# Attention's output accumulator in one PSUM bank, with three narrow products per token tile in place of a wide and a narrow one

## The chip, the cores and the metric

The kernel runs on one core of a Trainium2 chip. The metric is the device time of one execution in microseconds (us); three executions of the kernel before are shown, and one more that was profiled.

## What is computed

One block of a streaming encoder on 4096 tokens of width 1024: a normalisation, one projection, eight heads of causal attention with a forgetting gate (head width 64) beside four heads of chunkwise retention (head width 128), gates, an output projection, a second normalisation and the residual. The change touches the product of the attention weights with the values only:

```python
logits = jnp.einsum('bhqd,bhkd->bhqk', qb, kb) * scale
logits = logits + c[:, :, q0:q1, None] - c[:, :, None, :q1]
logits = jnp.where(kpos <= qpos, logits, -jnp.inf)
p = jax.nn.softmax(logits, axis=-1)
outs.append(jnp.einsum('bhqk,bhkd->bhqd', p.astype(vb.dtype), vb))
```

## The kernel before, in words

Matrix products run on TensorE in float16 with each operand split into a high and a low half, so that products of halves stand for a float32 product. The program order of every engine is written by Python generators; nothing is reordered afterwards. All results of TensorE go to tiles of one tag, `PS()`, with eight buffers, one for each bank of PSUM. A tile takes the bank that was given back first, and its first matmul waits until the last reader of the bank's former tile is done.

The stages: `phase_f0` (to about 400 us) projects for the first four heads. Then `attention()` runs over 64 items (8 heads by 8 blocks of 512 queries). Item (h, qb) has 4(qb + 1) steps, one for each 128 keys, 1152 steps in all. Between its steps the main loop puts pieces of other work, the fillers: the projection of the other four heads (`fill_f1`), the retention (`fill_r`) and the output projection (`fill_o`). Attention ends at about 2850 us and `fill_o` runs on alone.

A step of attention (lines 1116 to 1150) does this. Two matmuls make 128 keys by 512 queries of scores in a bank `st`; two banks are taken at a time, for two steps. ScalarE takes the exponential twice, as float32 (`pf`, L1140) and as float16 (`ph`, L1141); GpSimd subtracts them to `pl`, the low half (L308). `max_tile` (L983) computes scores of a later item once more in a bank of its own, and VectorE reduces them to row maxima `mrow` (L999); one or two such turns lie in each step. The step's `ph` and `pl` are queued in `pvq`.

In every fourth step, at `kt % 4 == 2`, `emit_pv` (L1046) is called four times and works off the four oldest entries. For each of the four tiles of 128 tokens it multiplies `pl` with 65 columns of the values `vt` (64 high halves and a column of ones, which sums the weights) and `ph` with all 129 columns (the 64 high halves, the ones, the 64 low halves). Each of these matmuls has its own weight load, since the attention weights are the stationary operand. Such a run of 32 matmuls is called a batch here. On the diagonal, where `i >= 0`, tiles before the i-th are left out: there a batch has 20 matmuls.

The results of an item accumulate in two banks, tiles 0 and 1 in the first, 2 and 3 in the second, at columns 0 and 256. An item's last batch holds its whole diagonal. When that batch has done `i == 1`, ScalarE copies the first bank to `ac` in SBUF, and at the last entry the second (L1070). Then `finish_item` (L1077) runs on VectorE: the reciprocal of the sums, the sum of the two 64-column parts, and the scaling. In the trace `ac` appears as `s`, and all of `tt` has the line L141, all of `mm` the line L104. The order of the work is set by costs that are written by hand: `emit_pv` counts as 88 for each tile of tokens (L1124), which the change leaves as it is.

Of the kernel before, what the change touches and what calls it, by code (L numbers as in the profile page):

```python
# [13 lines left out]
ALU = mybir.AluOpType  # L14
# [39 lines left out]
def kernel(  # L54
# [14 lines left out]
    nc = tc.nc  # L69
# [18 lines left out]
    def SB(tag, shape, dt=F32):  # L88
        cnt[0] += 1
        slot = SHARED.get(tag, tag)  # L90
        return sbp.tile(shape, dt, tag=slot, name=f"{tag}_{cnt[0]}", bufs=BUFS.get(slot, 1))

    def PS():
        cnt[0] += 1
        return psp.tile([128, 512], F32, tag="ps", name=f"ps_{cnt[0]}", bufs=8)
# [7 lines left out]
    def mm(o, lhsT, rhs, start, stop):  # L103
        nc.tensor.matmul(out=o, lhsT=lhsT, rhs=rhs, start=start, stop=stop, skip_group_check=True)  # L104

    def dma(o, i):
        nc.sync.dma_start(out=o, in_=i)  # L107
# [3 lines left out]
    def spawn(gen):  # L111

        if next(gen, None) is not None:
            chains.append(gen)
# [11 lines left out]
    def until(key):  # L126

        while key not in done:
            assert chains, key
            tick()  # L130

    def drain(gen):
        for _ in gen:
            pass
# [5 lines left out]
    def tt(o, a, b, op):  # L140
        nc.vector.tensor_tensor(out=o, in0=a, in1=b, op=op)  # L141

    def ts(o, a, s1, s2, op0, op1):
        nc.vector.tensor_scalar(out=o, in0=a, scalar1=s1, scalar2=s2, op0=op0, op1=op1)  # L144
# [776 lines left out]
    def load_ready():  # L921

        while cpos[0] < min(len(chunk_list), BUFS["kc"] + freed[0]) and is_stored(*chunk_list[cpos[0]]):
            load_chunk(*chunk_list[cpos[0]])
            cpos[0] += 1
# [21 lines left out]
    def load_x(n):  # L947
        if n >= len(items):
            return
        h, qb = items[n]  # L950
        while not is_stored(h, qb):
            push(h)
        xq = SB("xq", [128, 512], F16)
        dma(xq[0 : R2 + 64, :], QX[h, 0 : R2 + 64, qb * 512 : (qb + 1) * 512])
        xqs[n] = xq
        xloaded[n] = gstep[0]

    def load_lq(n):
        if n >= len(items):
            return  # L960
        h, qb = items[n]
        lq = SB("lq", [128, 512], F16)
        for w in range(2):
            dma(lq[(1 - w) * 64 : (2 - w) * 64], QX[h, R2 + w * 64 : R2 + (w + 1) * 64, qb * 512 : (qb + 1) * 512])
        z = SB("z1", [128, 4, 64])
        dma(z, ZD[h // 4][h % 4, :, 4 * qb : 4 * qb + 4, :])
        lqs[n] = (lq, z)
# [35 lines left out]
    def max_tiles(n):  # L1003

        while mdone[0] < len(mlist) and mlist[mdone[0]][0] <= n:
            max_tile()
            yield 1
# [27 lines left out]
    def attention():  # L1035
        load_ready()
        for n in range(4):
            if n not in xqs:
                load_x(n)
        if NB <= 4:  # L1040
            for n in range(2):
                load_lq(n)
                drain(max_tiles(n))
        pvq = []

        def emit_pv():  # L1046
            it, kt, i, ph, pl, first, last = pvq.pop(0)
            h, qb = items[it["n"]]
            _, vt = chunks_use[it["n"], kt]
            if first:  # L1050
                it["acc"] = [PS(), PS()]
            for t in range(max(0, i), 4):
                a = it["acc"][t // 2]
                o = (t % 2) * 256
                sl = slice(t * 128, (t + 1) * 128)
                v = vt[:, kt % 4, :]
                if first and t % 2 == 0:
                    mm(a[:, o : o + 129], ph[:, sl], v, True, False)
                    mm(a[:, o : o + 65], pl[:, sl], v[:, 0:65], False, i == t)
                else:  # L1060
                    mm(a[:, o : o + 65], pl[:, sl], v[:, 0:65], False, False)
                    mm(a[:, o : o + 129], ph[:, sl], v, False, i == t)
            if qb == NB - 1 and kt % 4 == 3:
                freed[0] += 1
            load_ready()
            if i == 1 or last:
                b = 0 if i == 1 else 1
                if b == 0:
                    it["ac"] = SB("s2", [128, 4, 129])
                nc.scalar.copy(  # L1070
                    out=it["ac"][:, 2 * b : 2 * b + 2, :],
                    in_=it["acc"][b].rearrange("p (t d) -> p t d", t=2)[:, :, 0:129],
                )
            if last:
                spawn(finish_item(it))

        def finish_item(it):  # L1077
            h, qb = items[it["n"]]
            ac = it["ac"]
            z = it["z"]  # L1080
            rec = SB("sm", [128, 4, 1])
            o = ac[:, :, 0:64]
            yield 1
            nc.vector.reciprocal(out=rec, in_=ac[:, :, 64:65])
            tt(o, o, ac[:, :, 65:129], ALU.add)
            yield 1
            ts(rec, rec, gsc[h // 4][1][:, KT + 2 : KT + 3], None, ALU.mult, ALU.bypass)
            tt(o, o, z, ALU.mult)
            yield 1
            tt(o, o, rec.to_broadcast([128, 4, 64]), ALU.mult)  # L1090
            for _ in range(3):
                yield 1
            dma(MX[qb][h // 2][:, :, (h % 2) * 64 : (h % 2) * 64 + 64], o)
            attn_done[h, qb] = True

        def max_rate(g):

            rate = 0.0
            for j in range(len(items)):
                if mdue[j] > mdone[0]:  # L1100
                    if j >= 4 and first_step[j - 4] > g + 16:
                        break
                    rate = max(rate, (mdue[j] - mdone[0]) / max(first_step[j] - LEAD - g, 1))
            return min(2, math.ceil(rate - 1e-9))

        chunks_use = {}
        mdue = [sum(4 * (items[i][1] + 1) for i in range(j + 1)) for j in range(len(items))]
        first_step = [0] + mdue
        for n, (h, qb) in enumerate(items):
            xq = xqs.pop(n)  # L1110
            lq, z = lqs.pop(n)
            it = dict(n=n, z=z)
            es = gsc[h // 4][0][:, KT + 4 : KT + 5]
            until(("m", n))
            steps = 4 * (qb + 1)
            for kt in range(steps):
                c, kk = kt // 4, kt % 4
                kc, vt = get_chunk(h, c)
                chunks_use[n, kt] = (kc, vt)
                cost = 0.0  # L1120
                if kt % 2 == 0:
                    if kt % 4 == 2 and len(pvq) >= 6:
                        for _ in range(4):
                            cost += 88 * (4 - max(0, pvq[0][2]))  # L1124
                            emit_pv()
                    sts = []
                    for j in (kt - 4 * qb, kt + 1 - 4 * qb):
                        p = PS()
                        if j >= 0:
                            mm(p[:, j * 128 : (j + 1) * 128], idb, maskT, True, False)  # L1130
                        sts.append(p)
                i = kt - 4 * qb
                q0 = max(0, i) * 128
                st = sts[kt % 2]
                mm(st[:, q0:512], kc[0 : R2 + 64, 1, kk * 128 : (kk + 1) * 128], xq[0 : R2 + 64, q0:512], i < 0, False)
                mm(st[:, q0:512], kc[:, 0, kk * 128 : (kk + 1) * 128], lq[:, q0:512], False, True)
                pf = SB("pf", [128, 512])
                ph = SB("ph", [128, 512], F16)
                pl = SB("pl", [128, 512], F16)
                nc.scalar.activation(out=pf[:, q0:512], in_=st[:, q0:512], func=AF.Exp, scale=es)  # L1140
                nc.scalar.activation(out=ph[:, q0:512], in_=st[:, q0:512], func=AF.Exp, scale=es)  # L1141
                ptt(pl[:, q0:512], pf[:, q0:512], ph[:, q0:512], ALU.subtract)
                pvq.append((it, kt, i, ph, pl, kt == 0, kt == steps - 1))
                cost += 2 * (512 - q0) * 0.42 + (56 if i >= 0 else 0)
                gstep[0] += 1
                for _ in range(max_rate(gstep[0])):
                    if max_ready():
                        max_tile()
                        cost += 216
                yield cost  # L1150
            drain(max_tiles(n + 1))
            load_x(n + 4)
            load_lq(n + 2)
        while pvq:
            emit_pv()
# [217 lines left out]
```

## Time and profile before

| | us |
|---|---|
| median of three executions | 3187.65 (3186.91 to 3191.37) |
| the profiled execution | 3185.68 |
| its span, first to last instruction | 3183.9 |
| TensorE busy | 3029.5 |
| VectorE busy | 2107.4 |
| ScalarE busy | 1889.9 |
| GpSimd busy | 1354.3 |

Engines: PE is TensorE's matmuls, PEld its weight loads, DVE is VectorE, ACT ScalarE, POOL GpSimd. A name with its operands reads out<-in. Matmuls are pipelined, so the duration of one (some 0.19 us for 65 columns) is longer than the distance from its start to the next one's start. The distance is what a run of them costs.

### The profile page before, as it was taken

To read this page: it belongs to the slowest core of one execution; us is meant where nothing else is said; L and a number is where in the kernel's file an instruction comes from. 1 tells how busy PE (TensorE), PEld (TensorE's weight loads), DVE (VectorE), ACT (ScalarE), POOL (GpSimd) and SP (SyncE) were. 2 spreads that over 40 slices of the span, in tenths; PEclk is the share of its full clock that TensorE was granted. 3 is DMA by queue.
4 is the path that set the end of the run, shared out by engine and by line. 5 is a ranking of instruction groups with operands and counts; after the bars stand their busy time and mean duration, and the time that the engine had idled before them with its cause. 6 is when DMAs were issued, how large, how long until landed. Compare 5 with 4: busy or idle time off the path is not lost.

```text
span 3183.9 us, 59454 instructions
## 1 busy us (share of the span) xinstructions
PE 3029.5 (95%) x22574; PEld 1780.5 (56%) x22575; DVE 2107.4 (66%) x4436; ACT 1889.9 (59%) x3572; POOL 1354.3 (43%) x1285
## 2 busy tenths in 40 slices
PE   8999989999999999999999998999999999889999
PEld 6667545555555555565555554555555555555554
DVE  6545577446556676777778768676867786645555
ACT  4333346676677666666667675667666766663332
POOL 0000024564555555555555564456445645550000
PEclk9999999999999999999999999999999999999999
DMA  6446743233244321211114122112111321124443
GB/s 188 144 163 162 201 112 90 67 86 91 65 104 119 78 61 53 65 51 53 59 54 106 46 83 85 52 39 82 55 38 44 110 62 43 56 67 139 139 139 119
DMA packets 266143, 284.10 MB, mean 89 GB/s; under 512 B 58976, under 2 KB 212192, under 8 KB 265856
## 3 DMA queue, kind: packets, MB, share of 16 engines
q1 hardware_dynamic: 265856, 280.30, 30.8%
q8 instruction: 177, 2.90, 0.4%
q14 instruction: 110, 0.90, 0.1%
HBM read 194.88 MB, written 88.74 MB: 89 GB/s over the span
## 4 chain that ended last, share of the span: by engine, by line
PE 75%; DVE 14%; issue 3%; ACT 3%; DMA 2%; POOL 2%; SPq 1%; POOLq 0%; DVEq 0%; ACTq 0%
PE ps L104 73%; DVE mrow L999 3%; DVE s L141 3%; DVE s L144 2%; DVE sm L141 1%; POOL pl L308 1%; ACT ph L1141 1%; ACT pf L1140 1%; PE ps L1196 1%; DMA rw<-in_w_in_dram 1%; DVE sm L144 1%; PE ps L349 1%; SPq L107 1%; DVE s L147 1%; DVE sm L147 1%
## 5 line engine op out<-in xcount | busy, mean ns | idle before, releaser
L308 POOL TENSOR_TENSOR pl<-pf,ph 128x512 f16<-128x512 f32 (+3 forms) x1152 | 1283.9, 1119 | 1164.1 <-ACT ph L1141 885.8
L1140 ACT ACTIVATE pf<-ps,gsc 128x512 f32<-128x512 f32 (+3 forms) x1152 | 758.4, 658 | 714.1 <-PE ps L104 696.9
L999 DVE TENSOR_REDUCE mrow<-ps 128x1 f32<-128x512 f32 (+3 forms) x1152 | 717.4, 640 | 366.9 <-PE ps L104 355.9
L104 PE MATMUL ps<-wn,xh 128*128 128x512 f16 (+2 forms) x3840 | 855.7, 360 | 3.7 <-DVE qk L147 3.4
L1141 ACT ACTIVATE ph<-ps,gsc 128x512 f16<-128x512 f32 (+3 forms) x1152 | 753.7, 654 | 0.0
L104 PEld LDWEIGHTS <-xh 128*128 128x128 f16 x4608 | 449.9, 98 | 461.7 <-issue 36.2
L104 PE MATMUL ps<-xh,wt 128*128 128x512 f16 x2688 | 672.9, 383 | 5.0 <-DVE mrow L999 4.6
L104 PEld LDWEIGHTS <-wt 128*128 128x128 f16 x3168 | 310.3, 99 | 365.9 <-issue 38.4
L104 PE MATMUL ps<-xq,kc 99*128 99x512 f16 (+3 forms) x1152 | 421.0, 366 | 27.1 <-DVE mrow L999 11.2
L104 PE MATMUL ps<-kc,xq 99*128 99x512 f16 (+3 forms) x1152 | 384.9, 365 | 45.6 <-DVE mrow L999 34.2
L104 PE MATMUL ps<-vt,ph 128*128 128x129 f16 x4224 | 420.4, 222 | 5.5 <-DVE mrow L999 4.9
L104 PE MATMUL ps<-lq,kc 128*128 128x512 f16 (+3 forms) x1152 | 420.0, 365 | 0.0
L104 PE MATMUL ps<-vt,pl 128*128 128x65 f16 x4224 | 405.9, 195 | 13.5 <-POOL pl L308 13.3
L104 PEld LDWEIGHTS <-kc 128*128 128x128 f16 (+1 forms) x3072 | 288.2, 99 | 213.9 <-issue 27.9
L104 PEld LDWEIGHTS <-pl 128*128 128x128 f16 x4224 | 375.2, 99 | 57.3 <-POOL pl L308 22.3
L104 PEld LDWEIGHTS <-ph 128*128 128x128 f16 x4224 | 377.4, 98 | 31.8 <-issue 1.6
L141 DVE TENSOR_TENSOR s<-s,s 64x512 f32<-64x512 f32 (+1 forms) x256 | 259.2, 1013 | 29.8 <-ACT s L755 22.7
L308 POOL TENSOR_TENSOR sm<-sm,nhalf 128x4 f32<-128x4 f32 (+2 forms) x80 | 62.9, 787 | 352.7 <-DVE sm L144 311.2
L104 PEld LDWEIGHTS <-xq 99*128 99x128 f16 x1152 | 112.4, 99 | 140.3 <-issue 13.5
L104 PE MATMUL ps<-wt,xh 128*128 128x512 f16 x768 | 183.0, 379 | 0.0
L141 DVE TENSOR_TENSOR ps<-ps,maskM 128x128 f32<-128x128 f32 x256 | 75.0, 293 | 105.6 <-PE ps L104 104.6
L141 DVE TENSOR_TENSOR xh<-ps,xh 128x256 f16<-128x256 f32 (+1 forms) x128 | 70.1, 555 | 104.0 <-ACT xh L338 84.5
(121 smaller groups left out, 2587.4 us busy)
## 6 DMA issues: line engine op xcount, KB each, us to landing
xh<-XT SPq DMA_DIRECT2D x176, 256.0 KB
rw<-in_w_in_dram SPq DMA_DIRECT2D x104, 256.0 KB
xt<-in_x_dram SPq DMA_DIRECT2D x36, 512.0 KB
s<-MX SPq DMA_DIRECT2D x32, 512.0 KB
out_dram<-xt SPq DMA_DIRECT2D x31, 512.0 KB
s<-in_x_dram SPq DMA_DIRECT2D x28, 512.0 KB
VD<-s SPq DMA_DIRECT2D x16, 516.0 KB
vt<-VD SPq DMA_DIRECT2D x64, 129.0 KB
```

Source lines behind the costliest of these rows:

```text
L104: nc.tensor.matmul(out=o, lhsT=lhsT, rhs=rhs, start=start, stop=stop, skip_group_check=True)
L107: nc.sync.dma_start(out=o, in_=i)
L141: nc.vector.tensor_tensor(out=o, in0=a, in1=b, op=op)
L144: nc.vector.tensor_scalar(out=o, in0=a, scalar1=s1, scalar2=s2, op0=op0, op1=op1)
L147: nc.vector.scalar_tensor_tensor(out=o, in0=a, scalar=s, in1=b, op0=op0, op1=op1)
L308: nc.gpsimd.tensor_tensor(out=o, in0=a, in1=b, op=op)
L349: nc.tensor.transpose(p[:, t * 128 : (t + 1) * 128], xs[t][:, k * 128 : (k + 1) * 128], idf)
L999: nc.vector.tensor_reduce(out=mrow[:, t, c : c + 1], in_=p[:, 0:w], axis=AX.X, op=ALU.max)
L1140: nc.scalar.activation(out=pf[:, q0:512], in_=st[:, q0:512], func=AF.Exp, scale=es)
L1141: nc.scalar.activation(out=ph[:, q0:512], in_=st[:, q0:512], func=AF.Exp, scale=es)
L1196: nc.tensor.transpose(p[:, e * 128 : (e + 1) * 128], mxt[:, half * 4 + e, :], idf)
```

## The change

Per token tile the wide product with `ph` is split in two of 65 and 64 columns, and both add into the same 64 columns. The sum of the two parts, which VectorE made at the end of an item, is thus made in PSUM. Four tiles of 65 columns fit one bank, so an item has one accumulator bank and one copy out of it, at its end. The products with `ph` now always come ahead of the one with `pl`. The matmul that opens the bank is the first of tile 0.

```diff
             if first:
-                it["acc"] = [PS(), PS()]
+                it["acc"] = PS()
+            a = it["acc"]
             for t in range(max(0, i), 4):
-                a = it["acc"][t // 2]
-                o = (t % 2) * 256
+                o = t * 65
                 sl = slice(t * 128, (t + 1) * 128)
                 v = vt[:, kt % 4, :]
-                if first and t % 2 == 0:
-                    mm(a[:, o : o + 129], ph[:, sl], v, True, False)
-                    mm(a[:, o : o + 65], pl[:, sl], v[:, 0:65], False, i == t)
-                else:
-                    mm(a[:, o : o + 65], pl[:, sl], v[:, 0:65], False, False)
-                    mm(a[:, o : o + 129], ph[:, sl], v, False, i == t)
+                start = first and t == 0
+                mm(a[:, o : o + 65], ph[:, sl], v[:, 0:65], start, False)
+                mm(a[:, o : o + 64], ph[:, sl], v[:, 65:129], False, False)
+                mm(a[:, o : o + 65], pl[:, sl], v[:, 0:65], False, i == t)
             if qb == NB - 1 and kt % 4 == 3:
                 freed[0] += 1
             load_ready()
-            if i == 1 or last:
-                b = 0 if i == 1 else 1
-                if b == 0:
-                    it["ac"] = SB("s2", [128, 4, 129])
-                nc.scalar.copy(
-                    out=it["ac"][:, 2 * b : 2 * b + 2, :],
-                    in_=it["acc"][b].rearrange("p (t d) -> p t d", t=2)[:, :, 0:129],
-                )
+            if last:
+                it["ac"] = SB("s2", [128, 4, 65])
+                nc.scalar.copy(out=it["ac"], in_=a[:, 0:260].rearrange("p (t d) -> p t d", t=4))
             if last:
                 spawn(finish_item(it))
...
             nc.vector.reciprocal(out=rec, in_=ac[:, :, 64:65])
-            tt(o, o, ac[:, :, 65:129], ALU.add)
             yield 1
```

## Rows read from the trace of the kernel before

**Rows 1.** The page: busy us, share of the span, instructions; chain that ended last.
```profile
PE 3029.5 (95%) x22574; PEld 1780.5 (56%) x22575; DVE 2107.4 (66%) x4436; ACT 1889.9 (59%) x3572; POOL 1354.3 (43%) x1285
PE 75%; DVE 14%; issue 3%; ACT 3%; DMA 2%; POOL 2%; SPq 1%; POOLq 0%; DVEq 0%; ACTq 0%
```
**Rows 2.** Busy us (instructions) of each engine, PEclk, DMA by stage.
```profile
500.00:1100.00 600.00, 598.30 (x4668) 330.69 (x4667) 334.93 (x657) 415.64 (x766) 327.61 (x311) 1.00 0.32 86
1100.00:2840.00 1740.00, 1627.63 (x12963) 968.04 (x12962) 1288.82 (x2522) 1163.26 (x2157) 956.99 (x851) 0.98 0.22 62
```
**Rows 3.** TensorE's waits, 1100:2840: total us, times, longest us.
```profile
PE ps L104 <- DVE mrow L999: 53.9, 46, 4.8
PE ps L104 <- POOL pl L308: 12.7, 6, 5.2
PE ps L1196 <- ACT s L1188: 8.4, 1, 8.4
PE ps L104 <- DVE state L147: 7.0, 7, 2.9
PE ps L811 <- DVE mrow L999: 3.2, 1, 3.2
```
**Rows 4.** Groups by form, whole span: count | busy us, mean ns | idle before.
```profile
L104 PE MATMUL ps<-vt,ph 128*128 128x129 f16 x4224 | 420.4, 222 | 5.5 <-DVE mrow L999 4.9 <-ACT ph L1141 0.5
L104 PE MATMUL ps<-vt,pl 128*128 128x65 f16 x4224 | 405.9, 195 | 13.5 <-POOL pl L308 13.3
L141 DVE TENSOR_TENSOR s<-s 128x256 f32<-128x256 f32 x64 | 47.2, 738 | 0.0
L1070 ACT COPY s<-ps 128x258 f32<-128x258 f32 x128 | 45.3, 391 | 15.3 <-PE ps L104 13.2
```
**Rows 5.** Matmuls of `vt` by stage: length, busy us (instructions), PEclk, DMA.
```profile
500.00:1100.00 600.00, 110.90 (x2228) 1.00 0.32 86
1100.00:2840.00 1740.00, 306.16 (x6012) 0.98 0.22 62
```
**Rows 6.** Timeline of a batch and the fill after it: start us, us, engine.
```profile
1505.00 0.19 PE L104 MATMUL ps<-vt,pl 128*128 128x65 f16 x1
1505.00 0.10 PEld L104 LDWEIGHTS <-ph 128*128 128x128 f16 x1
1505.03 0.22 PE L104 MATMUL ps<-vt,ph 128*128 128x129 f16 x1
1505.09 0.19 PE L104 MATMUL ps<-vt,pl 128*128 128x65 f16 x1
...
1506.41 0.38 PE L104 MATMUL ps<-xq,kc 99*128 99x512 f16 x1
...
1507.07 2.75 PE L104 MATMUL ps<-wn,xh 128*128 128x512 f16 x12
1509.65 1.05 PE L104 MATMUL ps<-s,s 128*128 128x128 f32 x8
```
**Rows 7.** Timeline of the first entry of an item, with narrow products in succession.
```profile
1101.59 0.23 PE L104 MATMUL ps<-vt,pl 128*128 128x65 f16 x2
1101.66 0.27 PE L104 MATMUL ps<-vt,ph 128*128 128x129 f16 x2
1101.77 0.22 PE L104 MATMUL ps<-vt,pl 128*128 128x65 f16 x2
1101.83 0.22 PE L104 MATMUL ps<-vt,ph 128*128 128x129 f16 x1
```
**Rows 8.** Timeline of the longest wait for a bank; brackets: idle before, releaser.
```profile
2323.83 0.38 PE L104 MATMUL ps<-xq,kc 99*128 99x512 f16 x1
2326.59 0.68 DVE L999 TENSOR_REDUCE mrow<-ps 128x1 f32<-128x512 f32 x1
2329.47 0.38 PE L104 MATMUL ps<-xq,kc 99*128 99x512 f16 x1
2331.39 2.07 DVE L144 TENSOR_SCALAR s<-s,sm,sm 128x128 f32<-128x128 f32 x4
2334.10 0.68 DVE L999 TENSOR_REDUCE mrow<-ps 128x1 f32<-128x512 f32 x1
2334.84 0.59 PE L104 MATMUL ps<-kc,xq 99*128 99x512 f16 x1 [4.76 <-DVE mrow L999]
```

## The prediction

> **What bounds the kernel now.** I read the page first, then the busy time by stage, then TensorE's waits in the stages where it is not full, and last the timeline at the instructions that change. The page says that TensorE is busy 95% of the span and holds 75% of the chain that ended last, with VectorE far behind at 14% [rows 1]. The stages say more. From 500 to 1100 us TensorE is busy 598.3 of 600 us: there every nanosecond that a matmul gains or loses shows in the end, and nothing else does. From 1100 to 2840 us it is busy 1627.6 of 1740 us, so it idles 112 us, and its granted clock is 0.98 [rows 2]. Both of these can be won back there. About three in four of the matmuls that the change touches lie in this second stretch, 6012 of 8448, and 2228 in the first [rows 5, 4].
>
> The waits in the second stretch show one large cause: matmuls that wait for the reduction of the maxima, 53.9 us in 46 waits and one more of 3.2 us, 57 us in all [rows 3]. No matmul in these waits reads `mrow`, which goes to VectorE alone. What it waits for is the bank that the reduction was reading. So these 57 us are a shortage of free banks while VectorE, which works in order, is busy with something else. The longest one shows it [rows 8]: between a reduction at 2326.59 and the next at 2334.10 VectorE does retention work (the last piece 2.07 us), and TensorE stands 4.76 us.
>
> **The change part by part.**
>
> *The third product, on TensorE, on the path.* A batch of 32 matmuls, 16 pairs of 65 and 129 columns, begins at 1505.00 and the next matmul starts at 1506.41 [rows 6]: 1.41 / 16 = 0.088 us a pair. The narrow one takes 0.03 of it (1505.00 to 1505.03) and the wide one the rest, 0.058. After the change a tile has three narrow products of 65, 64 and 65 columns. Columns are equal, 194 before and after. What is added is a matmul and a weight load, 4224 of each [rows 4]. At 0.03 each the three cost 0.090 us, 0.002 more than the pair: 4224 x 0.002 = +8 us. Ends: below, only the columns count. Twelve products of 512 columns take from 1507.07 to 1509.65, 0.215 us each [rows 6], that is 0.42 ns a column, and 194 of them 0.0815 us: -0.0066 a tile, -28 us. Above, narrow products in succession are slower than one alone. The only place that has two in a row is the first entry of an item: two from 1101.59 to 1101.66 and two from 1101.77 to 1101.83 [rows 7], 0.035 and 0.03 each. Three at 0.035 are 0.105: +0.017 a tile, +72 us. I take +8, by the row of a narrow product in the middle of a batch, as it is a case of the same code with a weight load in front of it. The weight load starts with the matmul before it (1505.00 for the product at 1505.03) [rows 6] and was in time 0.03 us later, which is what every product of the changed batch asks of it.
>
> By the Trainium skill (TensorE: Matmul & The Clock Gate, Back-to-back issue gap) a sustained stream of pairs of weight load and matmul costs about 81 ns at 128 columns, so that more and narrower products would be a plain loss. The trace does not agree: the product of 129 columns has 0.058 us and the pair of products 0.088, about one such figure for both [rows 6]. By that rule the third product would be worth 0.081 x 4224 = 342 us, an estimate from the page; the sum does not use it.
>
> *The order within a tile.* `ph` comes first and `pl` third. Six waits for GpSimd's `pl` cost 12.7 us, the longest 5.2 [rows 3]; such a wait now starts two narrow products, 0.06 us, later, six times: nothing. The wait for `ph` on ScalarE becomes explicit; behind it stands the whole of TensorE's queue. But GpSimd's `pl` is made from `ph`, so whoever could pass the one wait before had passed the other.
>
> *One bank less for an item.* Six banks were left for everything else while an item accumulates; now seven. Between an item's last batch and the next item's first neither kernel holds an accumulator: 4 of 4(qb + 1) steps, 256 of 1152, so the gain exists in 78% of the steps. What is one bank worth? Each step takes two banks, one for scores and one for a maximum; the three steps from 2323.83 to 2329.47 [rows 8] last 1.88 us each, so TensorE gets about 0.94 us further before it stands. A wait shorter than that goes; a longer one loses that much. The mean is 57.1 / 47 = 1.2 us and the longest 4.8 [rows 3], so many are short; I take 0.7 us for each: 47 x 0.7 x 0.78 = 26 us. Some comes back: VectorE still has the same backlog, and TensorE, which no longer stood, meets it later. VectorE is busy 74% in the stretch [rows 2], so it catches up mostly; I take a third off: -18 us. Ends: 0 and -57. The early copy at `i == 1` freed the first bank ahead of the end before, by part of one batch, under 1.4 us [rows 6]; that is too little to change the term.
>
> *The addition that goes, on VectorE.* 64 x 0.738 = 47 us [rows 4], off TensorE's path except when a bank waits behind it. Some 34 us of it lie in the second stretch. VectorE is late for about 5 us before each of the 47 waits, as in the one shown, 235 of 1740 us or 14%: 34 x 0.14 = -5 us. Ends: 0 and -34.
>
> *The copy that goes, on ScalarE.* 128 copies of 258 columns become 64 of 260: 64 x 0.391 = 25 us less [rows 4]. ScalarE is busy 67% in the stretch [rows 2] and TensorE waits on it in one large wait only, at L1196 [rows 3], far from these copies. Nothing. If ScalarE were the bound it would be at most those 25 us.
>
> *The clock.* 0.98 over 1740 us is 35 us of lost clock [rows 2]; with two levels, 1.2 and 2.4 GHz, that is some 70 us at the lower one, and what came before is a matmul that stood for some us. Waits for banks are half of the idle 112 us, so about 17 us of the 35 are theirs; I take a quarter of that: -4 us. Ends: 0 and -17.
>
> Sum: +8 - 18 - 5 - 4 = -19 us against the profiled execution's 3185.7 (its span of 3183.9 and 1.8 us around it): 3166.7. The median lies 2 us higher than that execution, so I predict 3169.
>
> **The rivals.**
>
> *Narrow products don't keep their pace (slower).* A weight load or its issue binds when narrow products follow each other without a wide one between. For it: one of the two places in rows 7 shows 0.035, and nowhere are there more than two in a row, while now there are 48. Instructions would have to come every 0.015 us over a whole batch against 0.022 now. Against it: in the same rows the other two kept 0.03. Price at 0.035: +72 - 27 = +45 us, 3233. It decides from the point where the loss eats the gain of 27: 27 / 4224 = 0.0064 on 0.088, a product of 0.0315 us. In its strong form every product costs what the wide one costs now, 0.058, because the load in front of it takes that long: three are 0.174, 0.086 more, +363 us and some 3520. The 0.03 after each narrow product [rows 6] speaks against it; it gets 0.02 of this rival's 0.18. The Trainium skill's section named above states a rule of this kind.
>
> *The bank waits only move (no change).* VectorE's backlog, not the number of banks, limits: TensorE takes the seventh bank and stands for the same reduction, as a total of 57 us against a VectorE busy for 1289 us would allow. For it: in rows 8 the bank would have been used up within 1 us of 4.76. Against it: VectorE is idle a quarter of the stretch, and a backlog that ends is not made up. Then +8 - 5: 3191, within 0.2%. Chance 0.17.
>
> *The waits and the clock give all they can.* Full 0.7 us without the third taken off, -26, the clock -12, the addition -8, and the products +2: -44, 3144. Chance 0.10.
>
> *The change doesn't free a bank.* If some other tile sits in the bank that is freed for as long (a projection's bank is held over 24 matmuls and what lies between them), the depth for scores and maxima stays: like the rival before, and counted in it.
>
> **How the numbers follow.** The forecast gets 0.55, the others 0.18, 0.17 and 0.10. The forecast's own range is the products at 0.03 plus or minus a nanosecond (3 x 4224 x 0.001 = 13 us) and the bank term from -8 to -26: 3146 to 3192. With the better rival below and part of the slower one above, the range is 3140 to 3197. A measurement of this kernel can tell about 0.2%, 6.4 us, from no change. Faster by more: nearly all of the forecast and the better rival, and little of the moved waits: 0.63. Slower by more: most of the slower rival and a little of the moved waits: 0.18. Within: 0.19.
>
> **What would show it.** In the profile after: a batch with 48 matmuls in place of 32 that takes 1.40 to 1.48 us, three starts 0.03 apart; if it takes 1.55 or more, the first rival decides. From 500 to 1100 us as many microseconds more as the products cost, 2228 / 8448 of the whole, 2 us. TensorE's waits for L999 from 57 down to some 35 us in the same stage; if they stay near 57, the second rival. The addition's 64 rows gone, 64 copies in place of 128, and a granted clock of at least 0.98. Wrong would be also a wait of TensorE on ScalarE at `ph` that wasn't there, or a wait at the copy for the one accumulator.

## The result and the profile after

The median falls from 3188.2 to 3150.6 us. The ratio of the changed kernel to the one before is 0.9883, with an interval of 0.9865 to 0.99: 37 us less, on the predicted side, twice the predicted 19 and within the range. The profiled execution of the kernel after took 3151.84 us, with a span of 3150.0 at a mean granted clock of 0.985; before it was 0.981. One kernel's executions differ in this figure: 17 of the kernel before on one chip have 0.977 to 0.983, and take 3197 to 3185 us. So the clock of one execution says little, and means over executions are given beside it below.

The page after, engines and chain:

```profile
PE 3029.2 (96%) x26798; PEld 1794.7 (57%) x26799; DVE 2076.8 (66%) x4372; ACT 1873.1 (59%) x3508; POOL 1351.6 (43%) x1285
PE 80%; DVE 12%; ACT 3%; issue 2%; DMA 2%; POOL 1%; SPq 1%; POOLq 0%; DVEq 0%; ACTq 0%
```

TensorE has 4224 matmuls and weight loads more and is busy for the same time as before [rows 1], because two things cancel: the added products make it longer (3052.2 us in the kernel that has them alone, below), and less of its work runs at the lower clock. The 34 us that the span lost are its idle time. TensorE's waits from 1100 to 2840 us (total us, times, longest us) show what ended it:

```profile
PE ps L104 <- DVE mrow L999: 33.5, 34, 4.2
PE ps L1188 <- ACT s L1180: 8.8, 1, 8.8
PE ps L104 <- ACT ph L1133: 7.3, 2, 3.9
PE ps L104 <- POOL pl L308: 3.7, 5, 1.0
PE ps L811 <- DVE mrow L999: 0.9, 1, 0.9
```

The waits for a bank that a reduction was reading went from 57.1 us in 47 [rows 3] to about 35 in 35. The waits for `pl` fell from 12.7 to 3.7, and 7.3 us now stand at `ph`, which is the first operand in the new order. These two nearly cancel.

A batch after the change (start us, us, engine):

```profile
1505.29 0.23 PE L104 MATMUL ps<-vt,ph 128*128 128x65 f16 x2
1505.35 0.19 PE L104 MATMUL ps<-vt,pl 128*128 128x65 f16 x1
1505.38 0.22 PE L104 MATMUL ps<-vt,ph 128*128 128x65 f16 x2
...
1506.73 0.19 PE L104 MATMUL ps<-vt,pl 128*128 128x65 f16 x1
1506.76 0.38 PE L104 MATMUL ps<-xq,kc 99*128 99x512 f16 x1
```

The 48 products take 1506.76 - 1505.29 = 1.47 us, 0.031 each with a weight load in front of each. Before it was 1.41 us for 32 [rows 6]. So the pace held over a whole batch, at a price of 0.06 us a batch. There are 8448 / 32 = 264 batches' worth, hence about 16 us of TensorE more.

The last view compares equal work. The windows are cut where the same step of attention starts its `pl` on GpSimd, so that each kernel's first window holds the same 256 steps (the row that starts at the edge makes 257) and its second the same 768. Columns are the length, the busy us (instructions) of the `pl` subtractions, PEclk and DMA. Before, and then after:

```profile
575.40:1078.30 502.90, 276.62 (x257) 1.00 0.32 88
1078.30:2718.50 1640.20, 866.74 (x768) 0.98 0.22 63
```

```profile
576.00:1082.20 506.20, 276.54 (x257) 1.00 0.33 87
1082.20:2683.30 1601.10, 865.00 (x768) 0.99 0.23 64
```

In the first stretch, where TensorE was full [rows 2], the same work takes 3.3 us longer. In the second it takes 39.1 us less. That is the prediction's picture, a price everywhere and a gain only where banks were short, with both amounts larger.

### The profile page after: what moved, and what is told of

It is laid out like the page before. It is cut to its first block, busy times and chain, and to the rows that moved or that the text cites. A ratio compares the mean times of both kernels' runs of the same rounds, so it can differ in the third digit from the quotient of the medians.

```text
span 3150.0 us, 67744 instructions
## 1 busy us (share of the span) xinstructions
PE 3029.2 (96%) x26798; PEld 1794.7 (57%) x26799; DVE 2076.8 (66%) x4372; ACT 1873.1 (59%) x3508; POOL 1351.6 (43%) x1285
## 4 chain that ended last, share of the span: by engine, by line
PE 80%; DVE 12%; ACT 3%; issue 2%; DMA 2%; POOL 1%; SPq 1%; POOLq 0%; DVEq 0%; ACTq 0%
PE ps L104 77%; DVE mrow L999 3%; DVE s L141 2%; DVE s L144 1%; DVE sm L141 1%; DMA rw<-in_w_in_dram 1%; ACT ph L1133 1%; PE ps L1188 1%; ACT pf L1132 1%; SPq L107 1%; PE ps L349 1%; DVE sm L144 1%; DVE s L147 1%; POOL pl L308 1%; POOL sm L308 0%
## 5 line engine op out<-in xcount | busy, mean ns | idle before, releaser
L999 DVE TENSOR_REDUCE mrow<-ps 128x1 f32<-128x512 f32 (+3 forms) x1152 | 717.6, 641 | 356.9 <-PE ps L104 345.8
L104 PEld LDWEIGHTS <-ph 128*128 128x128 f16 x8448 | 423.9, 97 | 76.0 <-issue 8.0
L104 PE MATMUL ps<-vt,ph 128*128 128x65 f16 (+1 forms) x8448 | 433.8, 195 | 10.4 <-ACT ph L1133 7.3
L104 PE MATMUL ps<-vt,pl 128*128 128x65 f16 x4224 | 423.4, 193 | 3.8 <-POOL pl L308 3.8
L104 PEld LDWEIGHTS <-pl 128*128 128x128 f16 x4224 | 393.3, 99 | 5.1 <-POOL pl L308 4.7
L104 PEld LDWEIGHTS <-kc 128*128 128x128 f16 (+1 forms) x3072 | 281.9, 99 | 196.8 <-issue 22.2
```

The source lines that it names most:

```text
L999: nc.vector.tensor_reduce(out=mrow[:, t, c : c + 1], in_=p[:, 0:w], axis=AX.X, op=ALU.max)
```

## The experiments

Ratios are to runs of the kernel before on the same chip, and 0.001 is 3.2 us. Kernels are compared with each other by these ratios; the changed kernel has 0.9883. Each has an interval of 3 to 7 us to either side, so a difference of a few us between two kernels isn't clear of the noise. Three dots in a diff stand for lines left out.

**The third product alone.** Two banks, the low halves in columns of their own, addition and copies kept.

```diff
...
+                start = first and t % 2 == 0
+                mm(a[:, o : o + 65], ph[:, sl], v[:, 0:65], start, False)
+                mm(a[:, o + 65 : o + 129], ph[:, sl], v[:, 65:129], False, False)
+                mm(a[:, o : o + 65], pl[:, sl], v[:, 0:65], False, i == t)
```

> The kernel before with the split of the wide product alone: two banks, the low halves beside the high ones in columns of their own, the addition on VectorE and both copies kept. A batch after the change takes 1.47 us against 1.41 before; 8448 / 32 = 264 batches' worth at 0.06 make +15 us. Theory (the bank pays for everything): 3188 + 15 = 3203, a little less (3198 to 3203) where the slower products run beside waits for VectorE that shrink by as much. Rival (narrow products cost nothing on the path, TensorE's lost time lies in waits): 3185 to 3190.

Measured: 1.0045 (1.0032 to 1.0058), +14 us, as its theory had it. Equal work:

```profile
579.40:1086.50 507.10, 276.61 (x257) 1.00 0.32 87
1086.50:2737.40 1650.90, 867.04 (x768) 0.98 0.22 62
```

4.2 us more in the full stretch and 10.7 in the other. The product is paid in full, also beside the waits: TensorE's 53.9 us for L999 [rows 3] did not shrink but were 56.1 here.

```profile
PE ps L104 <- DVE mrow L999: 56.1, 51, 4.6
```

**The change without its bank.** Three products into the same columns and no addition, with two accumulators and two copies.

```diff
-                it["acc"] = PS()
+                it["acc"] = [PS(), PS()]
...
+                a = it["acc"][t // 2]
+                o = (t % 2) * 256
...
```

> The changed kernel with its bank undone: three narrow products that add into the same 64 columns, no addition on VectorE, but two accumulator banks (tiles 0 and 1, tiles 2 and 3) and two copies, as before. Theory (the freed bank brings the gain): slower than before, 3203 less some 5 us for the addition that is gone, so 3195 to 3201, and the step from here to the changed kernel, 45 to 50 us, is the bank's. Rival (the addition that is gone from VectorE brings the gain, because it stood ahead of the reductions that banks wait for): 3155 to 3170, and the bank is worth under 15 us.

Measured: 0.9974 (0.9964 to 0.9984), -8 us against the kernel before. Neither expectation was met. From the third product alone it is 0.0071 or 23 us to here, for the addition and the narrower copies. From here to the changed kernel it is another 0.0091 or 29 us, for the bank and the second copy. Equal work, and then the waits for L999 from 1100 to 2840 us:

```profile
578.40:1084.70 506.30, 276.18 (x257) 1.00 0.33 87
1084.70:2715.30 1630.60, 864.31 (x768) 0.99 0.23 63
```

```profile
PE ps L104 <- DVE mrow L999: 49.5, 46, 4.5
```

The second stretch goes 1650.9, 1630.6, 1601.1: 20 us for the addition, 30 for the bank. The waits go 56.1, 49.5, 33.5. The second copy shows in no wait of TensorE: for `ph`, which ScalarE makes as well, it waits 7.8 us here and 7.3 in the changed kernel.

The busy time of all engines in the second stretch, TensorE's first, splits the bank's 30 us. Here, and then in the changed kernel:

```profile
1084.70:2715.30 1630.60, 1554.51 (x15115) 927.92 (x15114) 1210.12 (x2370) 1088.31 (x2040) 895.04 (x798) 0.99 0.23 63
1082.20:2683.30 1601.10, 1542.73 (x15115) 924.68 (x15114) 1207.91 (x2370) 1085.00 (x1998) 895.69 (x798) 0.99 0.23 64
```

TensorE idles 76.1 us and 58.4, 17.7 less. The same 15115 matmuls also keep it busy for 11.8 us less. Most of that is the clock: by the traces it stood at its lower level (1.2 GHz) for 47.8 us of this stretch with two banks and for 30.8 in the changed kernel, and half of such time is lost, 23.9 and 15.4 us. Over all executions the mean clocks are 0.9821 (11) and 0.9848 (4), which comes to the same 9 us.

**The addition put back.** The changed kernel with one more addition of the same size in the same place; its sum is not used.

```diff
             o = ac[:, :, 0:64]
+            ac2 = SB("s2", [128, 4, 64])
             yield 1
             nc.vector.reciprocal(out=rec, in_=ac[:, :, 64:65])
+            tt(ac2, o, o, ALU.add)
```

> The changed kernel with one more addition of 128 x 256 on VectorE at the end of each item, in the place where the old one stood; its sum goes to a tile that nobody reads. Theory (the bank): 3150.6 + 5, 3151 to 3158. Rival (the addition): +20 to +34, 3170 to 3185.

Measured: 0.9931 (0.9916 to 0.9946), +15 us over the changed kernel, between the two expectations. The added operation takes 51.6 us in all, so under a third of it is paid even where a bank more is free. Its group, TensorE's waits for L999, the second stretch with its equal work, and the span with the mean granted clock:

```profile
L141 DVE TENSOR_TENSOR s<-s 128x256 f32<-128x256 f32 x64 | 51.6, 806 | 0.0
```

```profile
PE ps L104 <- DVE mrow L999: 39.4, 41, 4.2
```

```profile
1084.30:2699.80 1615.50, 1551.36 (x15115) 929.43 (x15114) 1226.24 (x2412) 1083.64 (x1998) 899.44 (x798) 0.99 0.23 64
```

```profile
core 0: 3168.9 us, clock 0.981
```

The waits grow by 6 us only, and so does the idle time of the second stretch, from 58.4 to 64.1. The stretch is 14.4 us longer. The rest is the clock: it stood at the lower level for 47.8 us of this stretch against 30.8, 8.5 us more lost. The clocks of this one execution, 0.985 and 0.981, would give 13 us over the span; the means over executions, 0.9848 (4) and 0.9823 (6), give 8.

The clock falls where TensorE stands. In the kernel before, it went down during the 4.76 us wait of [rows 8], PEclk being the last but two:

```profile
2330.00:2333.00 3.00, 0.07 (x1) 0.00 (x0) 2.89 (x6) 1.84 (x3) 2.28 (x3) 1.00 0.00 0
2333.00:2340.00 7.00, 5.16 (x39) 3.51 (x39) 3.28 (x7) 0.00 (x0) 0.00 (x0) 0.51 0.11 39
```

All 16 stretches at the lower level between 1100 and 2840 us of that trace, and all 11 of the changed kernel's, begin in a wait of TensorE or within 2 us behind one; not every wait brings one.

**The same addition later.** Twelve turns after the item's end, on constants.

```diff
             attn_done[h, qb] = True
+            for _ in range(12):
+                yield 1
+            ac2 = SB("s2", [128, 256])
+            tt(ac2, csb[:, 0:256], csb[:, 0:256], ALU.add)
```

> The changed kernel with one addition of 128 x 256 on VectorE for each item, as in add_back, but 12 turns after the item's end and on constants. Theory A (the amount of work on VectorE counts, wherever it stands): the same price as add_back, +12 to +18 over the changed kernel. Theory B (the place counts: at an item's end VectorE is already late): under +7.

Measured: 0.9884 (0.9867 to 0.99), no price that can be measured. The same two views:

```profile
PE ps L104 <- DVE mrow L999: 35.1, 34, 4.2
```

```profile
core 0: 3152.7 us, clock 0.986
```

VectorE was busy 2113.5 us in this kernel against 2076.8 in the changed one, and the addition took 41.3 us in all. So the amount alone isn't the price, and the place counts: theory B was met. That VectorE is late at an item's end fits the waits of the kernel before: from 1100 to 2840 us, 39 of the 57 us for L999 end within 20 us behind an item's reciprocal, in 47% of that time. The other 18 us lie elsewhere. The later addition differs in one more thing, as it reads constants and no step of the item stands behind it. That a longer end of an item is not itself the price is shown by the end moved later, below.

**One tile of four split.** Three tiles at 129 columns and one at 65 are 452 columns, so one bank does. The addition is needed for three tiles.

```diff
+                o = t * 129
+                if t < 3:
+                    mm(a[:, o : o + 129], ph[:, sl], v, start, False)
+                else:
+                    mm(a[:, o : o + 65], ph[:, sl], v[:, 0:65], False, False)
+                    mm(a[:, o : o + 64], ph[:, sl], v[:, 65:129], False, False)
...
+                nc.scalar.copy(out=it["ac"].rearrange("p t d -> p (t d)")[:, 0:452], in_=a[:, 0:452])
...
+            tt(ac[:, 0:3, 0:64], ac[:, 0:3, 0:64], ac[:, 0:3, 65:129], ALU.add)
```

> One accumulator bank, but only the last of the four tiles has its wide product split: three tiles at 129 columns and one at 65 are 452 columns and fit the bank. Three quarters of the added products go (some 15 x 0.75 = 11 us of TensorE), and three quarters of the addition on VectorE come back. Theory (the bank brings the gain, the third product is its price): faster than the changed kernel, 3140 to 3147. Rival (the addition brings the gain): slower than it, 3160 or more.

Measured: 0.9889 (0.9874 to 0.9903), the same as the changed kernel; neither expectation was met. It fits three quarters of the 14 us saved on TensorE and three quarters of the addition's 15 paid again, but this run doesn't separate the two, and its copy is longer as well (452 columns, 546 ns, against 260 and 387).

**That addition on GpSimd, and then everything at an item's end.**

```diff
+            ptt(ac[:, 0:3, 0:64], ac[:, 0:3, 0:64], ac[:, 0:3, 65:129], ALU.add)
```

> one_split_of_four with its addition of 128 x 192 on GpSimd. If the addition on VectorE is what it gave back (about 15 x 0.75 = 11 us) it comes to 3140 to 3145; if GpSimd's pl is delayed by it, 3155 or more.

> one_split_add_gpsimd with both multiplications on GpSimd as well, so that VectorE takes nothing back from GpSimd at an item's end. There VectorE stood 45.6 us in 38 waits for GpSimd's addition. Theory (that standing, not GpSimd's work, is what made it 21 us slower than with the addition on VectorE): below scaling_on_gpsimd, 0.981 to 0.984 of before, as three quarters of the third product are saved on top. Rival (GpSimd's time is the price: its pl comes later): 0.990 or more, and waits of TensorE for pl over 15 us.

Measured: 0.9956 (0.9942 to 0.9969) with the addition alone on GpSimd, 21 us slower than with it on VectorE; 0.9901 (0.9881 to 0.9921) with the two multiplications moved too, level with the addition on VectorE. VectorE's waits from 400 to 2860 us in the first of the two:

```profile
DVE s L141 <- POOL s L308: 45.6, 38, 2.3
```

VectorE's next step takes the sum, so it stood for GpSimd. GpSimd's addition takes 0.58 us itself, where such a wait is 1.2 us in the mean; at 1543.80 us in that trace it began right behind a `pl` of 1.16 us. Without that step back the loss is gone, but the expected gain did not come: in the second kernel TensorE waits 13.3 us for `pl`, where the changed one has 3.7.

```profile
PE ps L104 <- POOL pl L308: 13.3, 13, 2.3
```

The total is the rival's (0.990 or more), its waits are a little under the 15 us that it named. Between the two kernels lie 0.0055 or 17 us, for the standing and two multiplications together, so both theories hold in part; how much each is worth was not separated.

**Both multiplications on GpSimd, the end of an item later, and both.** These begin from the changed kernel.

```diff
-            tt(o, o, z, ALU.mult)
+            ptt(o, o, z, ALU.mult)
...
-            tt(o, o, rec.to_broadcast([128, 4, 64]), ALU.mult)
+            ptt(o, o, rec.to_broadcast([128, 4, 64]), ALU.mult)
```

> The changed kernel with the two multiplications at an item's end (128 x 256 each) on GpSimd in place of VectorE. Putting the addition back cost about a third of its duration. Theory (VectorE's work at an item's end is paid at that rate): the two take 64 x (0.44 + 0.71) = 74 us of VectorE, so 20 to 25 us less, 3125 to 3131. Rival (GpSimd, which makes pl, becomes late and TensorE waits for it): waits of TensorE for L308 over 15 us and a total of 3150 or more.

```diff
-            yield 1
+            for _ in range(4):
+                yield 1
             nc.vector.reciprocal(out=rec, in_=ac[:, :, 64:65])
```

> The changed kernel with the end of an item (reciprocal, scaling) 3 turns later in VectorE's queue. In the changed kernel VectorE stands 50 us in 12 waits for ScalarE's copy of the accumulator, and an addition at that place costs 15 us while one 12 turns later costs nothing. Theory (at an item's end VectorE stands in front of the reductions that free banks, and what follows the copy is late): the waits for the copy go, TensorE's waits for L999 fall below 30 us, total 10 to 20 us less, 3131 to 3141 on the scale where the changed kernel has 3150.6. Rival (those 50 us are VectorE being ahead of TensorE, in items where nothing waits for it): the waits go but the total stays at 3148 to 3154.

> The changed kernel with an item's end 3 turns later, as in finish_later, and both its multiplications on GpSimd, as in scaling_on_gpsimd. Theory (both take work away from the same place, where VectorE is late for the reductions; the multiplications gone, the place matters less): no more than the better of the two alone, 0.984 to 0.986 of before. Rival (the place and the amount are two costs): the gains add, 0.979 to 0.983.

Measured: 0.9846 (0.9828 to 0.9863) on GpSimd, 12 us less than the changed kernel and half of what was expected, with 7.6 us of waits for `pl`, half of what the rival named; 0.9859 (0.9837 to 0.9882) for the end later, which can't be told from the changed kernel and lies between its two expectations; 0.985 (0.9835 to 0.9864) for both, no more than GpSimd alone. VectorE's standing for the copy in the changed kernel (a group by form: count, busy us, mean ns, idle before and its releaser), and its wait over the span with the end later:

```profile
L1077 DVE RECIPROCAL sm<-s 128x4 f32<-128x4 f32 x64 | 10.7, 168 | 50.3 <-ACT s L1066 50.3
```

```profile
DVE sm L1078 <- ACT s L1066: 6.1, 2, 5.1
```

The 50 us of standing fell to 6 and the total followed by some 8 us, within the noise; TensorE's waits for L999 are 32.4 us against 33.5. So nearly all of that standing was VectorE being ahead of TensorE, and an item's end that comes later costs nothing that can be measured. Three turns did not bring the gain of a better place either: where between 3 and 12 turns an operation becomes free was not tried.

**The pace of the narrow products.** Two edits to the changed kernel: a second product of 65 columns, with a column of zeros behind the low halves, and the product with `pl` between the two with `ph`.

```diff
-                mm(a[:, o : o + 64], ph[:, sl], v[:, 65:129], False, False)
+                mm(a[:, o : o + 65], ph[:, sl], v[:, 65:130], False, False)
```

> The changed kernel with one column more in the second product: the values get a column of zeros behind the low halves, and the product with it has 65 columns, adding zeros to the sums. In the changed kernel the product of 64 columns takes 0.033 us from its start to the next, the ones of 65 take 0.029, so a batch takes 1.47 us. Theory (a product of 64 columns is too short to cover the weight load behind it, and the next product misses its turn): 0.029 with 65, a batch of 1.41 us, 264 batches' worth at 0.064 = 17 us less on TensorE, in the total 8 to 17 us less: 3134 to 3143 (of before 0.983 to 0.986). Rival (the load of another tile's weights, or the odd start of the low halves, costs it): 0.033 or more as now, batch 1.47 or more, total 3150 to 3155.

```diff
+                mm(a[:, o : o + 65], pl[:, sl], v[:, 0:65], False, False)
+                mm(a[:, o : o + 64], ph[:, sl], v[:, 65:129], False, i == t)
```

> The changed kernel with the order within a token tile ph (65 columns), pl (65), ph (64 columns, the low halves). In the changed kernel the product with the low halves takes 0.033 us to the next start, the others 0.029. Theory (two loads of the same ph tile in succession, then one of pl, cost 4 ns): all three at 0.029, a batch of 1.40 us, 264 batches' worth at 0.065 = 17 us less on TensorE, of which most shows in the total, 3135 to 3143 on the scale where the changed kernel has 3150.6. Rival (the product that reads the low halves is slow itself, or the load of the next tile's weights): 0.033 stays behind that product, batch 1.47 us, total 3148 to 3154.

Measured: 0.9874 (0.9857 to 0.9891) and 0.9877 (0.9858 to 0.9897), both the same as the changed kernel. A batch of the first, and a batch of the second:

```profile
1514.36 0.23 PE L104 MATMUL ps<-vt,ph 128*128 128x65 f16 x2
...
1515.84 0.38 PE L104 MATMUL ps<-xq,kc 99*128 99x512 f16 x1
```

```profile
1514.31 0.19 PE L104 MATMUL ps<-vt,ph 128*128 128x65 f16 x1
...
1515.78 0.38 PE L104 MATMUL ps<-xq,kc 99*128 99x512 f16 x1
```

They take 1.48 and 1.47 us where 1.41 and 1.40 were expected. In nanoseconds the trace's starts still show one product in three, the one with the low halves, at 33 to 34 from its start to the next, and the others at 29. Neither the length of that product nor the two loads of one `ph` tile in succession is the cause. Nor is it that it adds into the columns of the product before it: with the low halves in columns of their own (the third product alone) the trace has 34 for it. In all four the low halves start at column 65 of the values, and that was not varied. Why it takes longer stays open.

## Why the prediction was right, and where its terms were off

**Direction, and the rival that was priced as slower.** Narrow products did keep their pace: 0.031 us each over 48 in succession, under the 0.0315 from which the rival would have decided. That margin is thin only because the predicted gain was small; with the gain of 52 us that was measured, the rival would have had to reach 0.033. The Trainium skill's figure (TensorE: Matmul & The Clock Gate, Back-to-back issue gap) of about 81 ns for a pair of weight load and matmul at 128 columns does not hold here: the product of 129 columns took 0.058 us [rows 6], and 48 of 64 and 65 columns took 1.47 / 48 = 0.031 each.

**The third product.** +8 predicted, +14 measured. The step that was off took 0.03 for each of three products. In nanoseconds the pair took 57 + 29 = 86 before. Two of the three products take 29 as well, which would have cost nothing, but the one with the low halves takes 33 to 34, and 4224 x 0.004 = 17 us. The two decimals of the timeline could not show this.

**The bank.** The mechanism was right, and the term for the waits too: -18 predicted, and from the kernel with two banks to the changed one TensorE idles 17.7 us less, 16 of it in the waits for L999. The whole step is worth 29 us because the clock gave back 8.5 more; some 3 us have no account.

**The clock.** This is the term that was most off: -4 predicted, -15 measured (30.7 us lost in the second stretch before, 15.4 after), near its own end of -17. The step that failed is the quarter that was taken of the waits' share. Shorter waits gave back about half as much in clock as in waiting with the bank (8.5 and 17.7 us), and more than the waiting with the addition put back (8.5 and 5.7). No run changed the clock alone.

**The addition.** -5 predicted; with its clock it is -23 when it is taken away beside two banks and -15 when it is put back beside one, of which 12 and 6 us are idle time. The failed step is the 14%, which spread the additions evenly over the stretch as if any moment were as good as any other. They stand at an item's end, and an addition 12 turns later costs nothing that can be measured.

**Order, copies, ScalarE.** The waits for `pl` shrank by 9 us and those for `ph` grew from 1.5 to 7.3, so the sum is nothing, as predicted. But a wait at `ph` that wasn't there was one of the prediction's signs of being wrong, and it came: the step that whoever could pass the one wait had passed the other holds for the sum, not for each wait. The other sign, a wait at the copy, did not: VectorE stood 51.2 us for it before and 50.3 after, and no wait of TensorE names it. The copies were not separated: the steps of 23 and 29 us hold them with the addition and the bank.

**The sum, and luck.** The steps of +14, -23 and -29 are successive differences of one row of ratios, so that they add up to the -37 proves nothing. In the other order, with the addition still there, the bank is worth more: from the third product alone to the addition put back it is 0.0114 or 36 us, and the addition then 15. The forecast had half of the change: its cost was 6 us too small and its gain 25. The first error hid a part of the second; without it the time would have been near 3145, below the 3146 at which the forecast's own range ends. The rival in which waits and clock give all they can (3144, chance 0.10) came nearer to 3150.6 than the forecast of 3169, though with the bank's waits too large and the products too cheap. That the waits would only move is ruled out by 57 us becoming 35; about two fifths of them went, as the prediction's 35 had it.

## What to carry to other kernels

Where an engine that works in order frees the buffers of the one that bounds, look at the place in its queue before its load: an operation of 0.74 to 0.81 us cost a third to a half of itself at an item's end here, and nothing that could be measured 12 turns later. A wait of TensorE that is shortened can come back twice, in the wait and in the granted clock, so price both, and take the clock from many executions. Moving work to a third engine helps when it goes there for good: the two multiplications on GpSimd gave 12 us more (0.9846, the lowest ratio here), while one step whose result VectorE had to take back cost 21.

## What the runs showed of the hardware that was not expected

Matmuls of 64 and 65 columns, each with its own load of 128 x 128 weights, start every 0.031 us in succession, and the one with the low halves takes some 4 ns longer than the others for a reason that the experiments did not find. The same multiplication of 128 x 256 in float32 took 0.43 us on VectorE and 0.75 on GpSimd by one operand, and 0.71 and 0.67 by a broadcast one:

```profile
L141 DVE TENSOR_TENSOR s<-s,z 128x256 f32<-128x256 f32 x64 | 27.5, 429 | 0.0
L141 DVE TENSOR_TENSOR s<-s,sm 128x256 f32<-128x256 f32 x64 | 45.1, 705 | 1.6
```

```profile
L308 POOL TENSOR_TENSOR s<-s,z 128x256 f32<-128x256 f32 x64 | 47.9, 749 | 0.9 <-ACT s L1066 0.9
L308 POOL TENSOR_TENSOR s<-s,sm 128x256 f32<-128x256 f32 x64 | 43.0, 672 | 25.5 <-DVE sm L144 13.1 <-PE ps L104 9.2 <-DVE sm L147 0.3
```

The first pair is of the changed kernel, the second of the one with both on GpSimd.
